# Query granules and gathered rows share a six-buffer ring: one ring of six becomes a pool of five and a pool of one, and row work begins within the second query granule

## Chip, cores and metric

The kernel runs on one core of a Trainium2 chip. The metric is the device time of one execution in microseconds (us). Before the change three runs took 1511.29 to 1512.45 us, median 1511.89 us.

## What is computed

Two transformer-like blocks on 256 tokens of width 1024, all in fp32. The first block has a mixer and a mixture of 32 experts. The second has two attentions and ends with a layer that picks, for each token, 128 of 16384 experts by product keys (16 for each of 8 heads) and applies them. Only that last layer is touched by what the change is about:

```python
q = (xt @ w_q).reshape(t, PEER_HEADS, 2, PEER_HALF)
sc = jnp.einsum("thpc,hpnc->thpn", q, sub_keys)
top_s, top_i = lax.top_k(sc, PEER_TOPK)
...
best_s, best_pos = lax.top_k(cand_s, PEER_TOPK)
idx = jnp.take_along_axis(cand_i, best_pos, axis=-1)
gate = jax.nn.softmax(best_s, axis=-1)
...
uc = u[ic]
act = jnp.einsum("cd,ced->ce", xc, uc)
hid = jax.nn.gelu(act) * gc
return jnp.einsum("ce,ced->cd", hid, v[ic])
```

## The kernel before, in words

**Weights.** All large weights are cut into granules of 128 x 4096 fp32 (2 MiB). `src` lists them in the order of use: 8 for the first mixer, 96 for the experts (two gates, two ups, two downs for each pair of experts), 17 for the second block, of which the last four are the query granules (`w_q`). A granule's load is issued by SyncE (SP) in `pump` (L298) as soon as its buffer is known to be free; `free` (L318) counts granules whose last piece has been split. Buffers come from a ring of six (`ring`), beside which a ring of three (`ring2`) serves during the first eight pairs of experts.

**Splitting.** Outside the experts each granule is used in pieces of 128 x 512. `chunk` (L197) splits a piece in two float32r parts: ScalarE (ACT) rounds the high part (L163), VectorE (DVE) or GpSimd (POOL) subtracts for the low part (L164), and TensorE (PE) multiplies both (L233). Pieces are split two ahead of their use. A query granule has eight pieces, so its last piece is split while its sixth is multiplied, and the next granule's first piece one step later.

**The last layer.** Four query granules are worked off one after the other (loop at the end of `_body`, `projT`, L225; here called the first to fourth granule, i = 0 to 3 in the code). After each, `scores` (L1326, L1328) multiplies with the keys, and `best` and `choose` (DVE, in small pieces) find the rows to gather: 32 per granule for the first 128 tokens, then 128 for the other tokens. `step` (L1238) emits one such piece of work and calls `fetch`.

**Rows.** For each of the 256 choices a *row tile half* is gathered: for each of 128 tokens one row of `uv`, 8 KiB, in all 1 MiB. Two gathers fill one 2 MiB buffer of the ring. `fetch` (L1228) issues them from POOL. In the code before, row buffers follow the granules in the same ring of six, in ring order: the first row pair takes the place of the sixth last granule, and so on, so the number of row pairs in flight is three during the second granule, four in the third, five in the fourth, six after it.

**Places.** `places` handles one pair of gathers at a time, here called a place: `first` twice (DVE, L1266, 128 x 1024 product with a sum), then `second` for both: Gelu (ACT, L1271), gate (L1273) and a diagonal matrix (L1275) for each, and matmuls that add the weighted rows to the result in PSUM (PE, L1278). When the matmuls of a place are done, its buffer is free and POOL issues the next pair of gathers. There are 128 places. Before the change, the first place comes with the first step of the third granule: `alongside` puts one place behind each of the nine steps of the third and of the fourth granule, and all others follow the fourth.

```python
def drive(main, fill, per):
    acc = 0.0
    for _ in main:
        acc += per
        while acc >= 1:
            acc -= 1
            next(fill, None)
```

The order of the instructions on each engine is the order in which this program emits them; an engine waits at its first instruction whose operands are not ready.

Of the kernel before, what the change touches and what calls it, by code (L numbers as in the profile page):

```python
# [1 line left out]

# [1 line left out]

# [4 lines left out]
F32 = mybir.dt.float32  # L9
# [22 lines left out]
NRING = 6  # L32
NRING2 = 3
# [20 lines left out]
RQ = 1.6  # L54
# [9 lines left out]
def _body(tc, A, out, dbg):  # L64
# [3 lines left out]
    def pool(name, bufs, **kw):  # L68
        return tc.tile_pool(name=name, bufs=bufs, reuse_waits="tile", **kw)
# [6 lines left out]
    with ExitStack() as ctx:  # L76
# [201 lines left out]
# [8 lines that stand above are left out]
# [3 lines left out]
        n_pre = len(src)  # L289
# [3 lines left out]
        src += [A["w_in2"][0], A["w_kv"]] + [A["w_in2"][i] for i in range(1, 8)] + [A["w_pa"], A["w_pb"]]  # L293
        src += [A["w_out2"][i] for i in range(2)] + [A["w_q"][i] for i in range(4)]
        st = {"emitted": 0, "freed": 0, "got": 0, "tiles": {}, "cap": 2, "next2": 0}
        R2_END = n_pre + 5 * (NRING + NRING2)

        def pump():  # L298
            while st["emitted"] < len(src) and st["emitted"] < st["freed"] + (NRING + NRING2 if rg[1] is not None and n_pre + NRING <= st["emitted"] < R2_END + NRING else st["cap"]):
                i = st["emitted"]  # L300
                if rg[1] is None and n_pre + NRING <= i < n_pre + NRING + NRING2:
                    break
                p = rg[1] if rg[1] is not None and n_pre <= i < R2_END and (i - n_pre) % (NRING + NRING2) >= NRING else rg[0]
                w = p.tile([128, 4096], F32, tag="w", name="w")
                n = src[i].shape[1]
                for o in range(0, n, 1024 if i == 0 else n):
                    v = slice(o, o + (1024 if i == 0 else n))
                    nc.sync.dma_start(w[:, v], src[i][:, v])
                st["tiles"][i] = w
                st["emitted"] += 1  # L310
# [10 lines left out]
                st["freed"] += 1  # L321
            pump()

        rg = [None, None]
        ringctx = ExitStack()
        rg[0] = ringctx.enter_context(pool("ring", NRING, side="right"))
        psctx = ExitStack()
        psx[0] = psctx.enter_context(pool("ps", 8, space=PSUM))
        pump()
# [24 lines left out]
        with pool("p1", 1) as p1:  # L354
# [3 lines left out]
            nc.sync.dma_start(kc2, A["kconst2"])  # L358
            nc.sync.dma_start(rr, row(A["grows"], R_END))
            nc.sync.dma_start(ws, A["w_s"])  # L360
            st["cap"] = NRING
            pump()
            nT = pp.tile([128, 2, 8, T], F32R, tag="xh", name="nT")
            warm(WARM[0])
# [277 lines left out]


        r2x = ExitStack()
        rg[1] = r2x.enter_context(pool("ring2", NRING2, side="right"))
        pump()
        xh = pp.tile([128, 2, 2, D], F32R, tag="xh", name="xh")
        if True:
# [70 lines left out]
            with pool("p2b", 2) as q, pool("p2c", 1) as q1:  # L719
# [76 lines left out]
                for p in range(16):  # L796
                    if p == 8:
                        r2x.close()
                        overflow(tc, nc, A, Pp, Wt, most, xh, res, gc, ident, bank, evac)
                        py = pyx.enter_context(pool("py", 1, side="right"))  # L800
                        fg = py.tile([128, D], F32, name="fg")
                        nc.gpsimd.dma_start(fg, row(A["final_gain"], D))
                        yy = py.tile([128, 2, D], F32, name="yy")
                        ss2 = py.tile([128, 2, 2], F32, name="ss2")
# [8 lines left out]
                    for dst in (pg, pu):  # L813
                        w = [get(), get()]
# [407 lines left out]
        todo = []  # L1222
        chosen = [0]
        got = {}
        row_st = {"next": 0, "done": 0}

        def fetch():

            while row_st["next"] < min(256, chosen[0]) and len(src) + row_st["next"] // 2 < st["freed"] + row_st["done"] // 2 + NRING:
                k = row_st["next"]  # L1230
                w = rg[0].tile([128, 4096], F32, tag="w", name="w")
                for j in range(2):
                    tt, s = divmod(k + j, 128)
                    got[k + j] = rw = w[:, j * 2 * D:(j + 1) * 2 * D]
                    nc.gpsimd.indirect_dma_start(rw, None, A["uv"], bass.IndirectOffsetOnAxis(ap=ei[tt][:, s:s + 1], axis=0))  # L1235
                row_st["next"] += 2
# [93 lines left out]
        def keep(qT, h0):  # L1330
            def f(hh, b):
                evac(flat(qT[:, h0 + 2 * hh:h0 + 2 * hh + 2, :]), b, eng="a")
            return f

        for i in range(4):
            qT = pq2.tile([128, 4, T], F32, name="qT")
            if i == 0:
                run(projT(8, n4, keep(qT, 0), 2))
                scores(0, qT, (0, 1))
                todo.append(seq(best(0, 0, (0, 1)), choose(0, 0, 1)))  # L1340
                lo_eng[0] = [nc.gpsimd]
                drive(projT(8, n4, keep(qT, 2), 2), fill, RQ)
                scores(0, qT, (2, 3))
                todo.append(seq(best(0, 0, (2, 3)), choose(0, 1, 1)))

                for tt in range(2):
                    for hf in range(2):
                        nc.tensor.matmul(acc[tt][hf], ident, res[:, tt, hf * 512:(hf + 1) * 512], start=True, stop=False, skip_group_check=True)
                continue
            drive(projT(8, n4, keep(qT, 0)), al if i > 1 else fill, 1 if i > 1 else RQ)  # L1350
            lo_eng[0] = [nc.vector]
            scores(i, qT, range(4))
            todo.append(seq(best(0, i), choose(0, 2 * i, 2)))
# [166 lines left out]
```

## Time and profile before

| | us |
|---|---|
| median of three runs | 1511.89 |
| the profiled execution | 1514.62 |
| its span in the trace | 1512.6 |
| PE busy | 1287.3 (85%) |
| DVE busy | 791.4 (52%) |
| ACT busy | 502.4 (33%) |
| POOL busy | 473.0 (31%) |
| DMA, mean rate over the span | 351 GB/s |

Busy time is that of instructions of an engine; waiting is not in it. The span runs from the first to the last instruction of the profiled execution, and the trace counts time from its start. The trace's mean shares hide that the program has stages with different limits: the experts run from about 150 to 610 us, the second block's attentions to about 795 us, the query granules from about 796 to 960 us, and the remaining rows to the end.

### The profile page before, as it was taken

The numbers are of one execution on the slowest core, as the hardware profiler recorded it, in microseconds if no ns is written. First come the engines' busy times: TensorE is split into PE (matmuls) and PEld (weight loads), VectorE is DVE, ScalarE is ACT, GpSimd is POOL, SyncE is SP. The second block draws the span as 40 slices with busy tenths as digits, with TensorE's granted clock in tenths as the row PEclk, the third lists the DMA queues.
The fourth block names the chain that finished last, engine by engine and source line by source line (L and its number), as shares of the span: only waits on it lengthen the run. The fifth ranks groups of instructions, "written<-read, shape, count | busy, mean of one in ns | idle before, by whom it ended". The sixth has DMA issues, their size and how long they took to land.

```text
span 1512.6 us, 16176 instructions
## 1 busy us (share of the span) xinstructions
PE 1287.3 (85%) x5523; PEld 703.8 (47%) x5523; DVE 791.4 (52%) x1797; ACT 502.4 (33%) x1211; POOL 473.0 (31%) x379
## 2 busy tenths in 40 slices
PE   9899999999899998999997878887777597777776
PEld 7676344334344453888886544433222232222222
DVE  4766222222222222677578667799874454544444
ACT  6635111011010012546654433444433232323332
POOL 1211000000000001243116343455566556665661
PEclk9999999999999999999998999999999999999999
DMA  9526799999999999644334698899999999999995
GB/s 390 225 112 278 312 426 428 426 428 426 428 428 427 429 427 427 265 177 147 115 123 162 241 399 303 358 422 422 421 421 421 421 422 421 422 422 421 421 422 237
DMA packets 57747, 530.21 MB, mean 351 GB/s; under 512 B 6592, under 2 KB 6848, under 8 KB 9408
## 3 DMA queue, kind: packets, MB, share of 16 engines
q0 software_dynamic: 37936, 272.65, 44.0%
q1 hardware_dynamic: 19440, 256.35, 40.7%
q8 instruction: 45, 0.74, 0.2%
q14 instruction: 38, 0.31, 0.1%
q10 hardware_dynamic: 288, 0.16, 0.0%
HBM read 528.08 MB, written 1.05 MB: 350 GB/s over the span
## 4 chain that ended last, share of the span: by engine, by line
DMA 27%; PE 12%; DVE 10%; issue 5%; ACT 3%; POOL 2%; POOLq 0%; DVEq 0%; ACTq 0%
DMA w<-in_uv_dram,ei 27%; PE b L233 6%; DVE jk L1266 5%; PE acc L1278 2%; PE b L262 1%; PE b L246 1%; POOL w L1235 1%; DVE sl L164 1%; ACT sh L163 1%; PE b L1030 1%; ACT dg L1275 1%; DVE oh L1186 1%; PE b L1016 0%; DVE en L1192 0%; PE b L976 0%
## 5 line engine op out<-in xcount | busy, mean ns | idle before, releaser
L1278 PE MATMUL acc<-w,dg 128*128 128x512 f32 x1024 | 479.5, 614 | 158.5 <-ACT dg L1275 158.2
L1235 POOL DMA_INDIRECT w<-in_uv_dram,ei x256 | 355.7, 1389 | 294.6 <-DMA w<-in_uv_dram,ei 131.7
L1266 DVE SCALAR_TENSOR_TENSOR jk<-w,xr 128x1024 f32<-128x1024 f32 x256 | 313.0, 1223 | 191.6 <-DMA w<-in_uv_dram,ei 189.8
L1278 PEld LDWEIGHTS acc<-w,dg 128*128 128x128 f32 x1024 | 188.8, 193 | 438.4 <-ACT dg L1275 244.0
L817 PE MATMUL b<-w,xg 128*64 128x512 f32 x1024 | 238.0, 601 | 11.9 <-DMA w<-in_w_gate_dram 9.6
L164 DVE TENSOR_TENSOR sl<-w,sh 128x512 fp32r<-128x512 f32 (+1 forms) x185 | 128.7, 702 | 105.6 <-ACT sh L163 105.1
L1271 ACT ACTIVATE act<-act,rr_n 128x2 f32<-128x2 f32 x129 | 38.1, 295 | 398.7 <-DVE jk L1266 398.5
L163 ACT ACTIVATE sh<-w 128x512 fp32r<-128x512 f32 (+1 forms) x208 | 122.3, 603 | 110.5 <-PE b L233 70.9
L817 PEld LDWEIGHTS b<-w,xg 128*64 128x64 f32 x1024 | 86.0, 138 | 151.9 <-issue 126.7
L811 POOL TENSOR_TENSOR Dw<-Dw,Wt 128x256 f32<-128x256 f32 x16 | 9.9, 617 | 391.1 <-DVE Dw L810 391.1
L855 PE MATMUL b<-w,hT 128*64 128x512 f32 x512 | 115.8, 595 | 6.3 <-ACT hT L124 5.5
L233 PE MATMUL b<-nT,sh 128*128 128x256 f32 x576 | 107.1, 286 | 3.2 <-ACT sh L163 1.7
L1275 ACT ACTIVATE dg<-kc,act 128x128 f32<-128x128 f32 x256 | 102.8, 401 | 8.3
L233 PEld LDWEIGHTS b<-nT,sh 128*128 128x128 f32 x576 | 88.9, 189 | 9.4 <-issue 4.7
L780 DVE TENSOR_TENSOR res<-res,b 128x512 f32<-128x512 f32 x64 | 39.9, 681 | 100.9 <-PE b L778 100.9
L233 PE MATMUL b<-nT,sl 128*128 128x256 f32 x288 | 81.9, 284 | 3.1 <-DVE sl L164 2.9
L860 DVE SCALAR_TENSOR_TENSOR eo<-b,gs,eo 128x512 fp32r<-128x512 f32 x32 | 24.0, 750 | 114.0 <-ACT eo L859 111.3
L1273 ACT ACTIVATE act<-act,gt 128x1 f32<-128x1 f32 x256 | 73.4, 287 | 4.2
L855 PEld LDWEIGHTS b<-w,hT 128*64 128x64 f32 x512 | 41.4, 137 | 68.1 <-issue 56.2
L824 DVE TENSOR_TENSOR hs<-hs,b 128x512 f32<-128x512 f32 x16 | 11.0, 688 | 106.4 <-PE b L817 106.4
L859 ACT ACTIVATE eo<-b,gs 128x512 fp32r<-128x512 f32 x32 | 22.0, 687 | 114.2 <-PE b L855 87.6
L246 PE MATMUL b<-sh,nT 128*128 128x512 f32 (+1 forms) x192 | 58.3, 380 | 0.5 <-ACT sh L163 0.5
(373 smaller groups left out, 1411.0 us busy)
## 6 DMA issues: line engine op xcount, KB each, us to landing
w<-in_w_gate_dram SPq DMA_DIRECT2D x32, 2048.0 KB, 19.1
w<-in_w_up_dram SPq DMA_DIRECT2D x32, 2048.0 KB, 21.3
w<-in_w_down_dram SPq DMA_DIRECT2D x32, 2048.0 KB, 19.1
w<-in_w_in_dram SPq DMA_DIRECT2D x13, 2048.0 KB, 16.7
w<-in_w_out_dram SPq DMA_DIRECT2D x4, 2048.0 KB, 13.2
w<-in_w_q_dram SPq DMA_DIRECT2D x4, 2048.0 KB, 7.9
w<-in_uv_dram,ei POOLq DMA_INDIRECT x256, 19.1
w<-in_w_in_dram SPq DMA_DIRECT2D x4, 512.0 KB, 7.1
```

Source lines behind the costliest of these rows:

```text
L163: nc.scalar.activation(hi, src, AF.Copy)
L164: (eng or nc.vector).tensor_tensor(lo, src, hi.bitcast(F32), op=ALU.subtract)
L233: nc.tensor.matmul(dst, l[:, c * 128:(c + 1) * 128], x[:, r, k, :], start=(k == 0 and c % 2 == 0 and i == 0), stop=(k == nk - 1 and i == 2 ...
L246: nc.tensor.matmul(bs[tt][:, :n], x[:, l, k, tt * 128:(tt + 1) * 128], r[:, :n], start=(k == 0 and i == 0), stop=(k == 7 and i == 2))
L780: nc.vector.tensor_tensor(rs, rs, b, op=ALU.add)
L817: nc.tensor.matmul(dst[64 * j:64 * j + 64, :], xg[:, k, 2 * pr + j, :], w[j][:, k * 512:(k + 1) * 512], start=(k == 0), stop=(k == 7))
L855: nc.tensor.matmul(bh[half][64 * j:64 * j + 64, :], hT[:, f, 64 * j:64 * j + 64], w[j][:, f * 1024 + half * 512:f * 1024 + half * 512 + 51 ...
L1235: nc.gpsimd.indirect_dma_start(rw, None, A["uv"], bass.IndirectOffsetOnAxis(ap=ei[tt][:, s:s + 1], axis=0))
L1266: nc.vector.scalar_tensor_tensor(junk, got[k][:, 0:D], 1.0, xr[:, tt], op0=ALU.mult, op1=ALU.mult, accum_out=act[tt][:, s:s + 1])
L1273: nc.scalar.activation(v[:, j:j + 1], v[:, j:j + 1], AF.Copy, scale=gf[tt][:, s + j:s + j + 1])
L1275: nc.scalar.activation(dg, ident, AF.Copy, scale=v[:, j:j + 1])
L1278: nc.tensor.matmul(acc[tt][hf], dg, rw[:, D + hf * 512:D + (hf + 1) * 512], start=False, stop=(s + j == 127), skip_group_check=True)
```

## The change

The ring of six becomes a pool of five (`ring`) and a pool of one (`ring1`); the three of `ring2` stay. `pool_of` says which granule lives where: during the first 45 expert granules the pattern of nine is five, one, three; elsewhere every sixth granule lives in the one. Of the last six granules, four live in the five, and the last two (the third and fourth query granules) both live in the one, so the fourth can only be loaded when the third has been split. Row pairs live in the five; once all granules are freed, every sixth pair lives in the one. `space` decides from counts of freed granules and finished rows whether a buffer may be taken. And in the second granule the steps are driven otherwise: four steps with two pieces of choosing each, then the other four steps and the end with 0.7 places each, which makes three places.

```diff
+        N_THREE = 45
+
+        def pool_of(i):
+
+            j = i - n_pre
+            if 0 <= j < N_THREE:
+                return 2 if j % 9 > 5 else 1 if j % 9 == 5 else 0
+            if i >= len(src) - 6:
+                return 1 if i >= len(src) - 2 else 0
+            return 1 if (i if j < 0 else j - N_THREE) % 6 == 5 else 0
+
+        held = [[], [], []]
+        size = (NRING - 1, 1, NRING2)
+        row_st = {"next": 0, "done": 0}
+
+        def space(p):
+            if rg[p] is None:
+                return False
+            if len(held[p]) < size[p]:
+                return True
+            x = held[p][-size[p]]
+            return x < st["freed"] if x >= 0 else 2 * (-1 - x) + 2 <= row_st["done"]
 
         def pump():
-            while st["emitted"] < len(src) and st["emitted"] < st["freed"] + (NRING + NRING2 if ... else st["cap"]):
+            while st["emitted"] < len(src) and st["emitted"] < st["freed"] + st["cap"]:
                 i = st["emitted"]
-                if rg[1] is None and n_pre + NRING <= i < n_pre + NRING + NRING2:
+                p = pool_of(i)
+                if not space(p):
                     break
...
-        rg[0] = ringctx.enter_context(pool("ring", NRING, side="right"))
+        rg[0] = ringctx.enter_context(pool("ring", NRING - 1, side="right"))
+        rg[1] = ringctx.enter_context(pool("ring1", 1, side="right"))
...
-            st["cap"] = NRING
+            st["cap"] = NRING + NRING2
...
         def fetch():
 
-            while row_st["next"] < min(256, chosen[0]) and len(src) + row_st["next"] // 2 < st["freed"] + row_st["done"] // 2 + NRING:
+            while row_st["next"] < min(256, chosen[0]):
                 k = row_st["next"]
-                w = rg[0].tile([128, 4096], F32, tag="w", name="w")
+
+                p = 1 if st["freed"] == len(src) and k % 12 == 10 else 0
+                if not space(p):
+                    break
+                held[p].append(-1 - k // 2)
+                w = rg[p].tile([128, 4096], F32, tag="w", name="w")
...
-            drive(projT(8, n4, keep(qT, 0)), al if i > 1 else fill, 1 if i > 1 else RQ)
+            if i == 1:
+                main = projT(8, n4, keep(qT, 0))
+                drive(itertools.islice(main, 4), fill, 2)
+                drive(main, al, 0.7)
+            else:
+                drive(projT(8, n4, keep(qT, 0)), al, 1)
```

What moves in the order of the instructions, at three places. First SP, the loads of the query granules (before, then after; in brackets what a load waits for; `w_5603` and `w_6653` are the buffers of the fourth granule):

```order
L308 DMA w_4813<-in_w_out2_dram 128x4096 [waits DMAHW4_49,DVE_49]
L308 DMA w_5062<-in_w_q_dram 128x4096 [waits DMAHW5_49,DVE_49]
L308 DMA w_5296<-in_w_q_dram 128x4096 [waits DMAHW6_49,DVE_49]
L308 DMA w_5463<-in_w_q_dram 128x4096 [waits DMAHW7_49,DVE_49]
L308 DMA w_5603<-in_w_q_dram 128x4096 [waits DMAHW0_49,DVE_49]
```

```order
L331 DMA w_4816<-in_w_out2_dram 128x4096 [waits DMAHW4_49,DVE_49]
L331 DMA w_5065<-in_w_q_dram 128x4096 [waits DMAHW5_49,DVE_49]
L331 DMA w_5464<-in_w_q_dram 128x4096 [waits DMAHW7_49,DVE_49]
L331 DMA w_5466<-in_w_q_dram 128x4096 [waits DMAHW6_49]
L331 DMA w_6653<-in_w_q_dram 128x4096 [waits DMAHW5_49,DVE_49,Pool_49]
```

The order of the loads stays, but the fourth granule's now waits for the DVE split of the last piece of the third granule (`w_5466`).

Second POOL, from the first gathers to the end of the second granule (`sl` is the low part of a piece; before, then after):

```order
L1235 DMA w_6155<-in_uv_dram,ei0_5863 128x2048 x2
L164 TENSOR_TENSOR sl_6175<-w_5296,sh_6174 128x512
L164 TENSOR_TENSOR sl_6195<-w_5296,sh_6194 128x512
L164 TENSOR_TENSOR sl_6217<-w_5296,sh_6216 128x512
L164 TENSOR_TENSOR sl_6240<-w_5296,sh_6239 128x512
L164 TENSOR_TENSOR sl_6265<-w_5296,sh_6264 128x512
L164 TENSOR_TENSOR sl_6290<-w_5296,sh_6289 128x512
L1235 DMA w_6307<-in_uv_dram,ei0_5863 128x2048 x2
L164 TENSOR_TENSOR sl_6311<-w_5463,sh_6310 128x512
L164 TENSOR_TENSOR sl_6331<-w_5463,sh_6330 128x512
L1235 DMA w_6398<-in_uv_dram,ei0_5863 128x2048 x2
```

```order
L1263 DMA w_6159<-in_uv_dram,ei0_5864 128x2048 x2
L165 TENSOR_TENSOR sl_6179<-w_5464,sh_6178 128x512
...
L165 TENSOR_TENSOR sl_6278<-w_5464,sh_6277 128x512
L165 TENSOR_TENSOR sl_6294<-w_5464,sh_6293 128x512
L1263 DMA w_6324<-in_uv_dram,ei0_5864 128x2048 x2
L1263 DMA w_6327<-in_uv_dram,ei0_5864 128x2048 x2
L165 TENSOR_TENSOR sl_6333<-w_5466,sh_6332 128x512
L1263 DMA w_6364<-in_uv_dram,ei0_5864 128x2048 x2
L165 TENSOR_TENSOR sl_6371<-w_5466,sh_6370 128x512
L1263 DMA w_6407<-in_uv_dram,ei0_5864 128x2048 x2
```

Ahead of the second granule's splits there are now four pairs of gathers and not three, and four further pairs are issued before the third granule begins, where there was one.

Third ACT, the end of the second granule (`sh` is the high part of a piece, `qT` the granule's result, `sc` the scores, `act0` and `dg` belong to a place; before, then after):

```order
L163 ACTIVATE sh_6289<-w_5296 128x512
L163 ACTIVATE sh_6310<-w_5463 128x512
L163 ACTIVATE sh_6330<-w_5463 128x512
L124 ACTIVATE qT_6171<-b_6172 128x512
L124 ACTIVATE qT_6171<-b_6173 128x512
L1328 ACTIVATE sc_5887<-b_6352,rr_n4_5916 128x512
L1328 ACTIVATE sc_5887<-b_6358,rr_n4_5916 128x512
L163 ACTIVATE sh_6367<-w_5463 128x512
L1271 ACT_TABLE_LOAD
L1271 ACTIVATE act0_5867<-act0_5867,rr_n4_5916 128x2
```

```order
L164 ACTIVATE sh_6293<-w_5464 128x512
L1299 ACT_TABLE_LOAD
L1299 ACTIVATE act0_5868<-act0_5868,rr_n4_5917 128x2
...
L164 ACTIVATE sh_6332<-w_5466 128x512
L1299 ACTIVATE act0_5868<-act0_5868,rr_n4_5917 128x2
...
L164 ACTIVATE sh_6370<-w_5466 128x512
L125 ACTIVATE qT_6175<-b_6176 128x512
L125 ACTIVATE qT_6175<-b_6177 128x512
L1299 ACTIVATE act0_5868<-act0_5868,rr_n4_5917 128x2
...
L1356 ACTIVATE sc_5888<-b_6410,rr_n4_5917 128x512
L1356 ACTIVATE sc_5888<-b_6416,rr_n4_5917 128x512
L164 ACTIVATE sh_6425<-w_5466 128x512
```

Three places now stand before the scores of the second granule, the third of them between the copy of its result and the scores.

## Rows read from the trace of the kernel before

**Rows 1.** Page, the span in 40 slices: rate of the DMA.
```profile
GB/s 390 225 112 278 312 426 428 426 428 426 428 428 427 429 427 427 265 177 147 115 123 162 241 399 303 358 422 422 421 421 421 421 422 421 422 422 421 421 422 237
```
**Rows 2.** Busy time by stage: stretch, length, engines, PE clock, DMA share, GB/s.
```profile
818.00:841.00 23.00, 19.48 (x118) 17.23 (x117) 13.07 (x46) 6.90 (x13) 17.94 (x17) 0.85 0.80 308
841.00:901.00 60.00, 49.35 (x199) 29.41 (x198) 41.06 (x115) 25.89 (x64) 24.22 (x21) 0.97 0.81 315
901.00:960.00 59.00, 47.19 (x176) 26.96 (x174) 40.59 (x117) 22.31 (x58) 21.06 (x20) 0.94 0.88 347
975.00:1480.00 505.00, 379.66 (x822) 149.23 (x821) 313.79 (x712) 176.13 (x529) 299.02 (x206) 0.99 1.01 420
```
**Rows 3.** Timeline of POOL late in the rows: start, length, operation.
```profile
1138.15 1.87 POOL L1235 DMA_INDIRECT w<-in_uv_dram,ei  x1 [0.62 <-DMA w<-in_uv_dram,ei]
...
1143.12 1.87 POOL L1235 DMA_INDIRECT w<-in_uv_dram,ei  x1 [0.61 <-DMA w<-in_uv_dram,ei]
```
**Rows 4.** Timeline of ACT, second to fourth granule; in brackets the idle time before.
```profile
834.77 0.63 ACT L163 ACTIVATE sh<-w 128x512 fp32r<-128x512 f32 x1 [1.35 <-PE b L233]
...
838.43 1.31 ACT L124 ACTIVATE qT<-b 128x512 f32<-128x512 f32 x2
...
842.66 1.28 ACT L1271 ACT_TABLE_LOAD   x1
845.81 0.30 ACT L1271 ACTIVATE act<-act,rr_n 128x2 f32<-128x2 f32 x1 [1.87 <-DVE jk L1266]
...
846.46 0.40 ACT L1275 ACTIVATE dg<-kc,act 128x128 f32<-128x128 f32 x1
...
873.10 0.61 ACT L163 ACTIVATE sh<-w 128x512 fp32r<-128x512 f32 x1
...
879.36 0.61 ACT L163 ACTIVATE sh<-w 128x512 fp32r<-128x512 f32 x1
...
906.19 0.29 ACT L1271 ACTIVATE act<-act,rr_n 128x2 f32<-128x2 f32 x1 [4.98 <-DVE jk L1266]
```
**Rows 5.** Timeline of DVE, first step of the third granule.
```profile
842.67 0.69 DVE L164 TENSOR_TENSOR sl<-w,sh 128x512 fp32r<-128x512 f32 x1 [7.96 <-ACT sh L163]
843.28 1.22 DVE L1266 SCALAR_TENSOR_TENSOR jk<-w,xr 128x1024 f32<-128x1024 f32 x1
```
**Rows 6.** Timeline of POOL: first gather, sixth gather, splits of the second granule.
```profile
818.43 1.05 POOL L1235 DMA_INDIRECT w<-in_uv_dram,ei  x1 [0.16 <-DVE gt L1198]
...
825.46 0.94 POOL L1235 DMA_INDIRECT w<-in_uv_dram,ei  x1 [0.30 <-issue]
826.42 3.74 POOL L164 TENSOR_TENSOR sl<-w,sh 128x512 fp32r<-128x512 f32 x3
```
**Rows 7.** Timeline of PE: the second granule's last matmul.
```profile
838.83 0.28 PE L233 MATMUL b<-n,sl 128*128 128x256 f32 x1
```
**Rows 8.** Chain that ended last, in order of time: start, length, what.
```profile
690.06 3.06 PE b L233 x24
...
872.63 3.70 PE acc L1278 x8
891.05 7.13 PE acc L1278 x16
```
**Rows 9.** DMA issues: KB each, median us to landing; page, then 877.5 to 880 us.
```profile
w<-in_w_q_dram SPq DMA_DIRECT2D x4, 2048.0 KB, 7.9
w<-in_uv_dram,ei POOLq DMA_INDIRECT x2, 11.0
```
**Rows 10.** Timeline of SP and busy time by stage, before the experts.
```profile
121.08 7.75 SPq L308 DMA_DIRECT2D w<-in_w_down_dram  x2
150.00:155.00 5.00, 5.00 (x32) 3.73 (x33) 2.08 (x5) 1.23 (x4) 0.44 (x1) 0.87 0.02 7
```
**Rows 11.** Timeline of DVE: two casts of row numbers, 128 x 16.
```profile
816.96 0.17 DVE L1193 CAST ei<-en 128x16 int32<-128x16 f32 x1
...
826.43 3.77 DVE L1193 CAST ei<-en 128x16 int32<-128x16 f32 x1
```

More of the change, by code (lines that the diff above doesn't have):

```diff
@@ L1 @@
 from contextlib import ExitStack
+import itertools
 import numpy as np
@@ L295, in _body @@
         st = {"emitted": 0, "freed": 0, "got": 0, "tiles": {}, "cap": 2, "next2": 0}
-        R2_END = n_pre + 5 * (NRING + NRING2)
+        N_THREE = 45
[16 more added lines that the diff above has]
+            return x < st["freed"] if x >= 0 else 2 * (-1 - x) + 2 <= row_st["done"]
         def pump():
-            while st["emitted"] < len(src) and st["emitted"] < st["freed"] + (NRING + NRING2 if rg[1] is not None and n_pre + NRING <= st["emitted"] < R2_END + NRING else st["cap"]):
+            while st["emitted"] < len(src) and st["emitted"] < st["freed"] + st["cap"]:
                 i = st["emitted"]
-                if rg[1] is None and n_pre + NRING <= i < n_pre + NRING + NRING2:
+                p = pool_of(i)
+                if not space(p):
                     break
-                p = rg[1] if rg[1] is not None and n_pre <= i < R2_END and (i - n_pre) % (NRING + NRING2) >= NRING else rg[0]
-                w = p.tile([128, 4096], F32, tag="w", name="w")
+                held[p].append(i)
+                w = rg[p].tile([128, 4096], F32, tag="w", name="w")
                 n = src[i].shape[1]
@@ L322, in free @@
             pump()
-        rg = [None, None]
+        rg = [None, None, None]
         ringctx = ExitStack()
-        rg[0] = ringctx.enter_context(pool("ring", NRING, side="right"))
+        rg[0] = ringctx.enter_context(pool("ring", NRING - 1, side="right"))
+        rg[1] = ringctx.enter_context(pool("ring1", 1, side="right"))
         psctx = ExitStack()
@@ L644, in _body @@
         r2x = ExitStack()
-        rg[1] = r2x.enter_context(pool("ring2", NRING2, side="right"))
+        rg[2] = r2x.enter_context(pool("ring2", NRING2, side="right"))
         pump()
@@ L798, in _body @@
                         r2x.close()
+                        rg[2] = None
                         overflow(tc, nc, A, Pp, Wt, most, xh, res, gc, ident, bank, evac)
@@ L1224, in _body @@
         got = {}
-        row_st = {"next": 0, "done": 0}
         def fetch():
-            while row_st["next"] < min(256, chosen[0]) and len(src) + row_st["next"] // 2 < st["freed"] + row_st["done"] // 2 + NRING:
+            while row_st["next"] < min(256, chosen[0]):
                 k = row_st["next"]
-                w = rg[0].tile([128, 4096], F32, tag="w", name="w")
+                p = 1 if st["freed"] == len(src) and k % 12 == 10 else 0
+                if not space(p):
+                    break
+                held[p].append(-1 - k // 2)
+                w = rg[p].tile([128, 4096], F32, tag="w", name="w")
                 for j in range(2):
```

## Prediction

> **What bounds the kernel now.** The page's 40 slices come first: the DMA runs near 425 GB/s through the experts, falls to 115 to 240 in the attentions, and from slice 27 on is level at 421 to 422 until the last [rows 1]. So the end is set by gathers, and the question is when they become an unbroken stream. The busy times by stage answer it: in the second granule (818 to 841 us) the DMA is busy 0.80 of the time, in the third 0.81, in the fourth 0.88, and from 975 us on 1.01 [rows 2]. Late in the rows POOL issues one pair of gathers per 1143.12 - 1138.15 = 4.97 us, and each issue was released by an earlier gather's landing [rows 3]. A pair that is ahead when the stream becomes unbroken is therefore worth 4.97 us, and a microsecond by which this moment comes later costs a microsecond.
>
> What sets the pace until then is no engine's busy time: PE is busy 49.35 of 60 us, DVE 41.06, ACT 25.89 [rows 2]. The timelines show a ring of waits. DVE does `first` twice (1.22 us each) [rows 5], ACT then Gelu, gates and diagonals of the place and only behind them the high part of the next piece, DVE the low part (0.69) behind that [rows 5], and the next `first` stands behind the low part. High parts come 879.36 - 873.10 = 6.26 us apart [rows 4]. A place within a granule so costs some 6.3 us against the 4.97 that its gathers need: that is where the DMA's idle time in the third and fourth granule comes from.
>
> The trace is of an execution of 1514.62 us (span 1512.6), 2.7 above the median 1511.89. I work out a difference on the trace and add it to the median. A measurement can tell about 0.2% (3 us) from no change.
>
> **What the change gains.** Places are counted from 0. Before, 18 stand in the third and fourth granule, and the gather that opens the unbroken stream waits for the first place behind them (18). With six pairs in flight 24 pairs have been issued by then. Now 3 + 9 + 9 = 21 places stand in the granules; the fourth granule still reaches six in flight (five, and the one when the last granule is split), so 27 pairs have been issued. Gain: 3 x 4.97 = **14.9 us**, if place 21 came when place 18 came.
>
> **What it costs: three places in the second granule.**
> - POOL issues eight gathers and not six before that granule's splits. The six took from 818.43 to 826.40, 1.33 each [rows 6]; two more are 2.7 us, and PE waits for the split behind them. PE's sixth step, two steps (3.06 us [rows 8]) before the end at 839.1 [rows 7], moves from 836.0 to 838.7.
> - ACT's last high part of the granule moves from 834.77 to 837.5 and ends at 838.1; a table load of 1.28 follows, then Gelu, gate and diagonal, 1.05 us from the first to the second's start plus its length [rows 4]: PE starts place 0 at about 840.4. A place is 3.70 us on PE [rows 8], a step 1.53. Place 0, step 7, place 1, step 8: 840.4 + 3.70 + 1.53 + 3.70 + 1.53 = 850.9.
> - Place 2 stands behind the copy of the result (1.31) [rows 4] and its own 1.05, then 3.70: 857.0.
> - From the last matmul of a granule's last place to the next granule's first Gelu the trace has 891.05 + 7.13 = 898.2 to 906.19 [rows 4, 8], 8.0 us: scores, their copies, a split, the first search, `first` twice. So the third granule's first Gelu comes at 865.0. Before it comes at 845.81 [rows 4].
>
> The third granule begins **19.2 us** late. From there on the instructions are the same, nine places per granule. As lower end I take PE's time of the three places alone, 11.1 us, all else hidden; as upper end 19.2 plus six `first` of 1.22 that hide nowhere, 26.5. I take 19.2, since it is the sum of rows in the order in which the engines must run them.
>
> **The last granule's load.** It was issued in the attentions, long before use; now it waits for the low part of the third granule's last piece. That piece's high part stands behind the third granule's fifth place, ACT's next high part, 6.26 us later, is already the new granule's first. High 0.61 and low 0.69 leave 6.26 - 1.30 = 5.0 us for a load. A 2 MiB load of this line lands after 7.9 us with little beside it; gathers issued in the same stretch as this load land after up to 11.0 [rows 9]. That bounds the wait at 2.9 and 6.0 us; with a whole pair of gathers before it (4.97 more) at 11.0. I take 9.5 to land, midway between the two rows: a wait of **4.5 us**. Behind it on ACT stands the next place's Gelu, on DVE the low part and all later `first`, so nothing of the ring of waits goes on. PE has two steps and the last place left, and gathers already issued go on landing: this costs no bandwidth, only time to the stream.
>
> The Trainium skill, *DMA: Bandwidth & Descriptors*, Anatomy of one DMA, gives 2.0 us plus bytes over 436 GB/s, an estimate of 6.8 us for this load; its section Queues, rings and completion order says that the DMA engines take turns between SP's and POOL's queues packet by packet, so a load would share and not queue. By the fit alone the wait would be 1.8 us and the sum 2.7 lower; the 7.9 us row is what I hold to as the lower end.
>
> **What costs nothing.** The pool split also delays two early loads. The fourth expert granule takes its buffer from the sixth weight before the experts and now from the seventh: it goes out at 121.08 [rows 10], when the fifth went out before. From there the loads behind it follow within 8 us, and the DMA's idle stretch after them (0.02 busy in 150 to 155 us [rows 10]) takes up the one load more, 4.97 us at most. Later the patterns of nine and of six give each granule the buffer of the same predecessor as before. The second and third query granules are loaded a little later or together, in the attentions, where the DMA is at 115 to 240 GB/s [rows 1]. Of these I book 0, at most 5 if the idle stretch were gone.
>
> **Sum.** 19.2 + 4.5 - 14.9 = +8.8 us. On the median: 1511.9 + 8.8 = **1520.7 us**, slower.
>
> **Rivals.**
> - *Faster: the three places hide in waits.* From 834.7 to 842.67 DVE waits 7.96 us for ACT [rows 5], and the DMA idles a fifth of the second and third granule [rows 2]. If the places used only such waits, the lag would be PE's 11.1 us less some 4.5 in which PE stands still at the turn to the third granule (an estimate from its 49.35 of 60 us [rows 2], of which I give this turn under half), 6.6; with the low wait of 2.9: 6.6 + 2.9 - 14.9 = -5.4, 1506.5 us. It decides at the third granule's first Gelu: before 845.8 + 14.9 - 4.5 = 856.2 us the change gains. Against it: PE runs its instructions in order, and the eight steps, three places and the scores stand on it one behind the other.
> - *No change: the lag is some 15 us and the load lands early.* 15.0 + 2.9 - 14.9 = +3.0 at most, about 1513.
> - *Slower still: DVE and POOL in each other's way.* A cast that takes 0.17 us took 3.77 while POOL split three pieces, 826.42 to 830.16 [rows 6, 11]: DVE ended when POOL did. Now six `first` and the second choice stand on DVE while POOL splits the rest of the second granule and two pieces of the third. If each `first` cost its 1.22 us on the path once, 7.3 more: 1528.0. The Trainium skill, *SBUF — State Buffer*, Who interferes with whom, says that a DVE instruction with two inputs in SBUF contends with a GpSimd instruction that reads SBUF, the later one being blocked for the whole of the other; by that rule `first` is such an instruction and this rival holds, and the sum would be 16.1 rather than 8.8. Against it: POOL's splits are spread over the granule and PE, not DVE, is the longer line in it.
> - *Slower still: the load queues behind gathers.* Wait 11.0 instead of 4.5: 1527.2. For it: five pairs may be outstanding. Against it: in these granules the DMA is idle a fifth of the time [rows 2], so the queue is short.
>
> **How the numbers follow.** Forecast (1515 to 1526) 0.60; no change 0.14; faster 0.11; contention 0.10; queued load 0.05. Slower in all: 0.60 + 0.10 + 0.05 = 0.75. The range leaves out most of the faster case and the far ends of the two slower ones: 1510 to 1528 us. Its ends lie inside the extremes 11.1 + 2.9 - 14.9 = -0.9 and 26.5 + 11.0 - 14.9 = +22.6, which would need all unknowns on one side; the lower is stretched by a microsecond towards the faster rival.
>
> **What would show it.** In the new trace the three places' matmuls should lie between about 840 and 857 us and the third granule's first Gelu at 865; the DMA should be busy over 0.9 from 820 to 857 (0.80 before). On ACT a wait of 3 to 6 us for the fourth granule's load should stand behind the third granule's sixth place, near 898 us. The unbroken stream should begin near 998 us, 24 later than before, with 54 gathers behind it and not 48. The forecast is wrong if the first Gelu comes before 856 or no wait for the load is seen on ACT; it is wrong in its logic if the stream's start is as late as I say and the end is not.

## The result, and the profile after

After the change four runs took 1524.70 to 1525.13 us, median 1524.82; the kernel before, beside them, had a median of 1512.17. The ratio is 1.0082, with a 95% interval of 1.0064 to 1.0099: 12.65 us slower. The profiled execution took 1524.70 us (span 1522.9), 10.1 more than the profiled one of before, which lay 2.5 above its median. The forecast was 1520.7 us, slower, in 1510 to 1528.

In the profile after, everything up to the first gather of the rows is 1.8 us earlier than in the one of before (816.62 against 818.43 [rows 6]). Differences "from the first gather" below leave this offset out.

Rate by slices (page), and busy time by stage with the columns of [rows 2]:

```profile
GB/s 390 221 56 320 348 428 428 426 427 426 428 427 427 428 428 427 247 179 151 77 66 220 292 344 270 357 416 422 420 421 422 421 421 421 421 422 421 422 421 216
```

```profile
818.00:841.00 23.00, 15.63 (x85) 12.39 (x84) 18.89 (x47) 8.11 (x18) 20.58 (x15) 0.85 0.94 370
841.00:860.00 19.00, 13.32 (x69) 9.08 (x67) 4.17 (x16) 5.19 (x11) 8.50 (x9) 0.98 0.98 407
860.00:900.00 40.00, 32.66 (x120) 18.79 (x120) 25.91 (x81) 14.97 (x38) 12.80 (x12) 0.92 0.78 296
900.00:922.00 22.00, 14.19 (x35) 6.99 (x36) 10.96 (x19) 6.96 (x19) 4.27 (x5) 0.77 0.68 273
980.00:998.00 18.00, 12.49 (x38) 6.18 (x37) 13.59 (x61) 5.17 (x15) 5.81 (x6) 0.91 1.02 421
998.00:1490.00 492.00, 370.93 (x802) 145.40 (x800) 309.58 (x711) 172.38 (x518) 287.69 (x202) 0.99 1.01 421
```

The DMA is busy 0.94 to 0.98 up to 860 us, where it was 0.80 [rows 2]; it falls to 0.78 and 0.68 in the third granule and is unbroken (1.02) only from about 980 us on. The timeline of ACT shows why; it answers to [rows 4]: the three new places' Gelus, the third granule's first and sixth, the first split of the fourth granule, the seventh Gelu, the fourth granule's first:

```profile
836.30 0.29 ACT L1299 ACTIVATE act<-act,rr_n 128x2 f32<-128x2 f32 x1
...
838.40 0.28 ACT L1299 ACTIVATE act<-act,rr_n 128x2 f32<-128x2 f32 x1
...
847.94 0.29 ACT L1299 ACTIVATE act<-act,rr_n 128x2 f32<-128x2 f32 x1
...
860.75 0.30 ACT L1299 ACTIVATE act<-act,rr_n 128x2 f32<-128x2 f32 x1 [4.98 <-DVE jk L1294]
...
893.26 0.30 ACT L1299 ACTIVATE act<-act,rr_n 128x2 f32<-128x2 f32 x1 [4.07 <-DVE jk L1294]
...
900.96 0.63 ACT L164 ACTIVATE sh<-w 128x512 fp32r<-128x512 f32 x1 [6.03 <-DMA w<-in_w_q_dram]
...
906.70 0.29 ACT L1299 ACTIVATE act<-act,rr_n 128x2 f32<-128x2 f32 x1 [5.11 <-DVE jk L1294]
...
930.89 0.29 ACT L1299 ACTIVATE act<-act,rr_n 128x2 f32<-128x2 f32 x1 [4.99 <-DVE jk L1294]
```

Two late points stand in it. The third granule's first Gelu comes 44.13 us after the first gather (860.75 - 816.62) and not 27.38 [rows 4, 6]: a lag of **16.8 us**. And the third granule is 70.14 us long (to 930.89), not 60.38 [rows 4]: **9.8 us** more, most of it at 900.96, where ACT waits 6.03 us for the fourth granule's load. PE's clock goes down behind the wait: 0.77 in 900 to 922 us. On SP the load goes out at 889.97 us, and right behind it the load of the last norm's gain, which before had been issued at 769 us:

```profile
889.97 0.33 SPq L331 DMA_DIRECT2D w<-in_w_q_dram  x1
890.49 0.33 SPq L1389 DMA_DIRECT2D fg<-in_norm_f_dram  x1
```

Last, the issues of gathers. In the kernel before, the pair that opens the unbroken stream (24, counted from 0) and the last gather:

```profile
971.50 1.53 POOL L1235 DMA_INDIRECT w<-in_uv_dram,ei  x1 [11.49 <-PE acc L1278]
...
1480.21 1.88 POOL L1235 DMA_INDIRECT w<-in_uv_dram,ei  x1 [0.61 <-DMA w<-in_uv_dram,ei]
```

After the change (pair 27, and the last):

```profile
995.06 1.74 POOL L1263 DMA_INDIRECT w<-in_uv_dram,ei  x1 [10.02 <-DVE cand L1183]
...
1488.82 1.88 POOL L1263 DMA_INDIRECT w<-in_uv_dram,ei  x1 [0.61 <-DMA w<-in_uv_dram,ei]
```

The stream opens 23.56 us later with three pairs more issued. 23.56 - 3 x 4.97 = 8.65, and the last gather is 8.61 us later: the lateness of the stream's start less the pairs that are ahead is the whole difference up to there. Only the span behind the last gather is not in this account: 34.1 us here, 32.4 before. The 1.7 us lie in the last 16 matmuls, which take 8.83 us here and 7.13 before; the granted clock is 0.69 in 1506 to 1511 us, where it was 1.00 in that place before (1498 to 1506 us). In the four kernels of the next part that hold parts of the change the span behind the last gather is 32.4 to 32.5 us, but in the changed kernel with another order of splitting it is 34.2, with the same 8.83. Whether these 1.7 us belong to the change or to single executions is open.

### The profile page after: what moved, and what is told of

It is laid out like the page before. It is cut to its first block, busy times and chain, and to the rows that moved or that the text cites. A ratio compares the mean times of both kernels' runs of the same rounds, so it can differ in the third digit from the quotient of the medians.

```text
span 1522.9 us, 16160 instructions
## 1 busy us (share of the span) xinstructions
PE 1291.2 (85%) x5523; PEld 700.9 (46%) x5523; DVE 791.1 (52%) x1797; ACT 502.3 (33%) x1211; POOL 468.0 (31%) x379
## 4 chain that ended last, share of the span: by engine, by line
DMA 28%; PE 13%; DVE 9%; issue 5%; ACT 3%; POOL 2%; POOLq 0%; DVEq 0%; ACTq 0%; SPq 0%
DMA w<-in_uv_dram,ei 28%; PE b L234 6%; DVE jk L1294 4%; PE acc L1306 3%; PE b L263 1%; PE b L247 1%; POOL w L1263 1%; DVE sl L165 1%; DMA w<-in_w_q_dram 1%; ACT sh L164 1%; DVE en L1217 1%; PE b L1055 1%; DVE oh L1211 1%; ACT dg L1303 0%; PE b L1041 0%
## 5 line engine op out<-in xcount | busy, mean ns | idle before, releaser
L1306 PE MATMUL acc<-w,dg 128*128 128x512 f32 x1024 | 485.1, 620 | 164.4 <-ACT dg L1303 164.0
L1263 POOL DMA_INDIRECT w<-in_uv_dram,ei x256 | 346.6, 1354 | 313.2 <-DMA w<-in_uv_dram,ei 123.8
L842 PEld LDWEIGHTS b<-w,xg 128*64 128x64 f32 x1024 | 82.7, 139 | 155.1 <-issue 132.7
```

The costliest lines, as they stand in the source:

```text
L842: nc.tensor.matmul(dst[64 * j:64 * j + 64, :], xg[:, k, 2 * pr + j, :], w[j][:, k * 512:(k + 1) * 512], start=(k == 0), stop=(k == 7))
L1306: nc.tensor.matmul(acc[tt][hf], dg, rw[:, D + hf * 512:D + (hf + 1) * 512], start=False, stop=(s + j == 127), skip_group_check=True)
```

## The experiments

The theory when they began: the three early places cost about what they win; the loss comes from the fourth granule's late load. The rivals: the places themselves, or DVE and POOL in each other's way. All medians stand beside runs of the kernel before on the same chip; the experiments ran in three groups, in which it took 1512.75, 1511.98 and 1513.25 us.

### The pools alone

```diff
-            if i == 1:
-                main = projT(8, n4, keep(qT, 0))
-                drive(itertools.islice(main, 4), fill, 2)
-                drive(main, al, 0.7)
-            else:
-                drive(projT(8, n4, keep(qT, 0)), al, 1)
+            drive(projT(8, n4, keep(qT, 0)), al if i > 1 else fill, 1 if i > 1 else RQ)
```

> The pools of five and one as changed, but no places in the second granule: it is driven as before (1.6 pieces of choosing per step), the first place comes with the third granule. Theory (the loss is the last granule's late load; three early places cost about what they gain): the wait for that load stays, 6 us on ACT behind the third granule's sixth place, with some 2.6 us of slower TensorE after it, and no pair is gained: 24 pairs at the start of the unbroken stream. The third granule's first Gelu is 0 to 3 us later than before (two more gathers on POOL ahead of the splits). About 1512.2 + 9.8 = 1522 us, 1519 to 1525. Rival (the loss is the lag that the early places make): without them about the time before, 1511 to 1515 us, the wait for the load being taken back by the gathers that go on landing meanwhile.

Measured: 1523.52 us, ratio 1.0081 (1.0062 to 1.0100). ACT's timeline (the third granule's first Gelu, the fourth's first split):

```profile
846.50 0.29 ACT L1299 ACTIVATE act<-act,rr_n 128x2 f32<-128x2 f32 x1 [1.87 <-DVE jk L1294]
...
887.66 0.63 ACT L164 ACTIVATE sh<-w 128x512 fp32r<-128x512 f32 x1 [7.53 <-DMA w<-in_w_q_dram]
```

The third granule begins on time (26.5 us from the first gather, 820.04, against 27.4) and is 69.45 us long. Without a single early place all of the loss is there: the pools alone cost what the whole change costs.

### The places alone

The kernel before, its ring of six kept:

```diff
-            drive(projT(8, n4, keep(qT, 0)), al if i > 1 else fill, 1 if i > 1 else RQ)
+            if i == 1:
+                main = projT(8, n4, keep(qT, 0))
+                drive(itertools.islice(main, 4), fill, 2)
+                drive(main, al, 0.7)
+            else:
+                drive(projT(8, n4, keep(qT, 0)), al, 1)
```

> The ring of six of the kernel before, with the new driving of the second granule: three places in it, the fourth granule's load issued long before use. Theory: no wait for a load; the third granule's first Gelu comes some 17 us later against its first gather, 27 pairs stand at the start of the stream: 16.8 - 14.9 = +1.9 us against before, 1514 us, 1512 to 1517 (the upper end if the longer tail, 1.7 us, belongs to the places). Rival (the places themselves lose, by contention of DVE and POOL or by an order that hides nothing): 1520 to 1525 us. Second rival (with three pairs in flight instead of four in the second granule the third place has its gathers late): the first Gelu of the third granule over 20 us later than before.

Measured: 1516.07 us, ratio 1.0016 (1.0006 to 1.0027), +2.4 us by the ratio. ACT's timeline, the third granule's first, sixth and seventh Gelu:

```profile
860.57 0.30 ACT L1273 ACTIVATE act<-act,rr_n 128x2 f32<-128x2 f32 x1 [4.99 <-DVE jk L1268]
...
893.63 0.29 ACT L1273 ACTIVATE act<-act,rr_n 128x2 f32<-128x2 f32 x1 [4.08 <-DVE jk L1268]
...
900.93 0.30 ACT L1273 ACTIVATE act<-act,rr_n 128x2 f32<-128x2 f32 x1 [5.11 <-DVE jk L1268]
```

From the first gather (818.36) the first Gelu comes after 42.21 us, a lag of 14.8, against a gain of 14.9: the three places cost what they gain. Most of the +2.4 lies inside the third granule, which is 61.99 us long, 1.6 more than before. The sixth and the seventh Gelu are 7.30 us apart here and 13.44 after the change: the difference, 6.14, is ACT's wait for the load (6.03). The lag is 2 us shorter than after the change; six gathers and not eight stand ahead of the splits on POOL here.

### The last granule in the five, and the gain's load first

The first of these two keeps the third granule in the one and puts the fourth into the five, so that it loads early; a pool's held buffers are counted, so that rows may pass the granules:

```diff
-                return 1 if i >= len(src) - 2 else 0
+                return 1 if i == len(src) - 2 else 0
...
-            if len(held[p]) < size[p]:
-                return True
-            x = held[p][-size[p]]
-            return x < st["freed"] if x >= 0 else 2 * (-1 - x) + 2 <= row_st["done"]
+            return sum(x >= st["freed"] if x >= 0 else 2 * (-1 - x) + 2 > row_st["done"] for x in held[p]) < size[p]
```

> As changed, but only the third granule lives in the one; the fourth is loaded into the five, early. A pool's buffers are counted as free when fewer than its number are held, whatever their order. One pair fewer is in flight in the second, third and fourth granule (three, four, four instead of four, five, five). Theory: no wait for the fourth granule's load, the third granule is 60 and not 70 us long: 1524.8 - 9.8 = 1515 us, 1513 to 1518. Rival (four pairs in flight are too few for a place per 6.3 us, so what the load gives back the gathers take): the first places of the fourth granule wait for gathers and the time stays above 1520 us.

Measured: 1515.31 us, ratio 1.0020 (1.0012 to 1.0029). Taking the late load away gives back 9.4 us of the 12.65 (1.0082 - 1.0020 of 1512), although one pair fewer is in flight, and the lag is 14.0 (first Gelu at 860.77, first gather at 819.43). Its profiled execution (1520.15 us) lies 4.8 above its own median, with a place of 6.72 us on PE in the third granule; I read no lengths of that granule from it.

The second moves the load of the last norm's gain (`fg`, two lines) ahead of the loop over the granules:

> As changed, but the load of the last norm's gain (512 KB), which stands on SP directly behind the fourth granule's late load, is issued ahead of that load, before the query granules are worked off. Theory: the two loads shared the DMA; alone the granule lands up to 0.5 MB / 421 GB/s = 1.2 us earlier: the wait on ACT is 4.8 to 5.6 us and not 6.0, the time 1523.5 to 1524.5 us. Rival (the load is slow by the gathers beside it and its own length alone): wait and time as they are, within 0.3 us.

Measured: 1524.33 us, ratio 1.0082 (1.0069 to 1.0096). SP's and ACT's timelines:

```profile
806.25 0.33 SPq L1364 DMA_DIRECT2D fg<-in_norm_f_dram  x1
...
888.98 0.33 SPq L331 DMA_DIRECT2D w<-in_w_q_dram  x1
```

```profile
899.29 0.63 ACT L164 ACTIVATE sh<-w 128x512 fp32r<-128x512 f32 x1 [5.35 <-DMA w<-in_w_q_dram]
```

The wait is 5.35 and not 6.03 us: 0.7 shorter, within the theory's 4.8 to 5.6. The medians, 0.5 us apart, are too near to tell.

### What sets the pace in the granules

The prediction had said that a ring of waits does: DVE's `first`, ACT's Gelu and behind it the next high part, DVE's low part, the next `first`. Five kernels try it. Three have the next piece split between the two `first` and the Gelu (the body of `chunk`'s loop becomes `split_next`):

```diff
+        def split_ahead():
+            if cs["i"] < len(cs["q"]) and len(cs["ready"]) <= cs["look"]:
+                cs["ready"].append(split_next())
...
                         first(k + i)
+                    split_ahead()
                     second(k + j, n)
```

On the kernel before:

> The kernel before, with one change of order: within a place, the next piece of the query granule is split (high part on ACT, low part on DVE) between the two first and the Gelu, not behind the Gelu, gates and diagonals. Theory (a place within a granule costs 6.3 us because ACT's high part stands behind the Gelu, which waits for both first, and DVE's low part waits for that high part; PE needs only 3.70 + 1.53 = 5.23): DVE no longer waits for ACT, a place costs 5.2 to 5.5 us, the 18 places of the third and fourth granule take some 18 x 0.9 = 16 us less, the unbroken stream begins that much earlier: 1512.2 - 16 = 1496 us, 1493 to 1504. Rival (PE or the landing of the gathers sets the pace of the places): 1509 to 1514 us. Second rival (the high part, now ahead of the Gelu, delays the place's matmuls by its 0.6 us and takes back what it gives): 1510 to 1516 us.

With the ring of six and the three early places:

> The ring of six of the kernel before, the new driving with three places in the second granule, and the split between the two first and the Gelu. Theory: the gain of that order as in the kernel before with it, and three places at about their price: within 3 us of the run of the kernel before with that order, 1494 to 1505 us. Rival (three early places pay once the granules are faster, since PE is then the bound and a place costs 5.2 us against the 4.97 us of its gathers): no, they would then lose up to a microsecond less; below that run by more than 3 us would show that the lag in the second granule came from the same order of ACT and DVE.

On the kernel as changed:

> The kernel as changed, with the split between the two first and the Gelu. Theory: the fourth granule's load is still issued only when the third granule's last piece is split and still needs some 10 us to land; the place that hides part of it is shorter, so the wait is 6 to 8 us; the places gain as in the other kernels with that order: 8 to 12 us above the run with the ring of six, the new driving and that order. Rival (the wait for the load came of the order of ACT and DVE): within 4 us of that run.

Measured: 1521.17 (ratio 1.0057, 1.0043 to 1.0071), 1522.40 (1.0072) and 1534.09 us (1.0143). My expectation failed: the order made all three slower. Of the comparisons among the three, those that were expected hold: the places cost 1.2 us, the late load another 11.7. ACT's wait for that load is 9.37 us in the third of them, longer than the 6 to 8 expected. ACT's timeline of the first shows what happened:

```profile
859.13 0.28 ACT L1278 ACTIVATE act<-act,rr_n 128x2 f32<-128x2 f32 x1
...
865.28 0.63 ACT L163 ACTIVATE sh<-w 128x512 fp32r<-128x512 f32 x1 [4.48 <-PE b L240]
865.81 0.28 ACT L1278 ACTIVATE act<-act,rr_n 128x2 f32<-128x2 f32 x1
```

There are three buffers for high parts; with one more piece kept ready the new one takes the buffer of the step that PE has just been given, so ACT waits 4.48 us for that step, and the Gelu stands behind it: a place costs 6.68 us. The fourth kernel takes the low parts of the last two granules from DVE instead:

```diff
-            lo_eng[0] = [nc.vector]
             scores(i, qT, range(4))
```

> The kernel before, with the low parts of the third and fourth granule on POOL instead of DVE. Theory (the ring of waits of ACT and DVE sets the pace): DVE's first no longer wait for the low parts, PE sets the pace with 5.2 us per place, 1496 to 1506 us, if POOL's low parts (1.3 us each) leave DVE alone. Rival (DVE and POOL are in each other's way): a first beside a low part of POOL takes up to twice its 1.22 us and POOL's issues of gathers stand behind its low parts, 1512 to 1520 us.

Measured: **1493.95 us**, ratio 0.9877 (0.9860 to 0.9893). That leaves two readings (order, or less work on DVE), so the kernel before with `split_ahead` was tried again, with a piece less kept ready:

```diff
+            if i > 1:
+                cs["look"] = 1
             drive(projT(8, n4, keep(qT, 0)), al if i > 1 else fill, 1 if i > 1 else RQ)
```

> The kernel before with the next split between the two first and the Gelu, as in the earlier run with that order, but in the third and fourth granule one piece fewer is kept ready, so that the split finds one of the three buffers free and ACT's high part does not wait for the step just ahead of it on PE. Theory (the ring of waits from DVE's first over ACT's high part to DVE's low part sets the pace, and the earlier run lost only because the high part waited 4.48 us for PE's step, with the Gelu behind it): 4.9 to 5.3 us per place, as with the low parts on POOL, 1493 to 1500 us. Rival (taking the low parts from DVE was what helped, its busy time and not the order): 6 us per place and more, 1508 to 1516 us.

Measured: **1493.90 us**, ratio 0.9875 (0.9858 to 0.9892). The low parts are still on DVE, and the gain is the same: DVE's load need not fall for it, the new order is enough. What keeping one piece fewer ready does without the new order was not run. Timelines of PE, with the low parts on POOL, and of ACT and the stages, with the new order:

```profile
865.09 3.60 PE L1278 MATMUL acc<-w,dg 128*128 128x512 f32 x8
...
869.95 3.60 PE L1278 MATMUL acc<-w,dg 128*128 128x512 f32 x8
```

```profile
863.16 0.30 ACT L1278 ACTIVATE act<-act,rr_n 128x2 f32<-128x2 f32 x1 [2.00 <-DVE jk L1273]
...
868.11 0.29 ACT L1278 ACTIVATE act<-act,rr_n 128x2 f32<-128x2 f32 x1 [2.07 <-DVE jk L1273]
```

```profile
841.00:860.00 19.00, 18.64 (x76) 11.08 (x75) 18.69 (x67) 10.47 (x26) 8.78 (x7) 1.00 0.73 271
860.00:900.00 40.00, 36.10 (x144) 21.37 (x143) 32.41 (x98) 17.38 (x46) 17.71 (x17) 0.96 1.01 416
900.00:925.00 25.00, 25.00 (x108) 15.41 (x107) 23.05 (x44) 13.04 (x32) 13.68 (x13) 1.00 1.01 417
```

A place comes every 4.86 us with the low parts on POOL and every 4.95 with the new order (868.11 - 863.16), PE has no gap between places in the last stretch (25.00 of 25 us busy), and the DMA is full from 860 us on and not from 975. Both beat the kernel before by 18 to 19 us; the two changes weren't joined.

### The changed kernel and its places at this pace

Low parts on POOL (the same line left out), first with the ring of six and the early places, then in the kernel as changed:

> The ring of six, the new driving with three places in the second granule, and the low parts of the third and fourth granule on POOL. Theory: with a place per 4.9 us the gathers are the bound from the third granule on, so a place more in the second granule moves no gather but those ahead of the turn; the eighth pair is issued at 868.4 us with the ring of six and these places, at 864.1 us in the kernel before with low parts on POOL: 1494 + 4 = 1498 us, 1494 to 1502. Rival (27 pairs instead of 24 at the stream's start are worth their 14.9 us whatever the pace): 1483 to 1490 us.

> The kernel as changed, with the low parts of the third and fourth granule on POOL. Theory: the wait for the fourth granule's load is still there on ACT (5 to 8 us), but with a place per 4.9 us five pairs in flight are mostly not landed yet, some 20 us of gathers, so the DMA does not idle and the wait costs nothing at the end: 1493 to 1499 us, no later than the ring of six with the same places and low parts on POOL. Rival (the wait adds its length whatever the pace): 7 to 10 us above that run, 1503 to 1509 us.

Measured: 1496.06 us (ratio 0.9890, 0.9872 to 0.9909) and 1512.28 us (0.9997, 0.9988 to 1.0006). The first is as the theory had it, 2.1 above the kernel without early places. For the second the theory failed; the wait does add its length, as the rival had it, but it is 15.78 us long, and the late load costs 16.2. ACT's and POOL's timelines:

```profile
902.80 0.63 ACT L164 ACTIVATE sh<-w 128x512 fp32r<-128x512 f32 x1 [15.78 <-DMA w<-in_w_q_dram]
```

```profile
887.25 0.95 POOL L1263 DMA_INDIRECT w<-in_uv_dram,ei  x1 [0.83 <-PE acc L1306]
888.50 0.94 POOL L1263 DMA_INDIRECT w<-in_uv_dram,ei  x1 [0.30 <-issue]
889.46 1.27 POOL L165 TENSOR_TENSOR sl<-w,sh 128x512 fp32r<-128x512 f32 x1
```

The third granule's last low part now stands on POOL behind two gathers that waited for PE; the buffer is free at 890.7, 3.7 us after ACT had come to the next piece (887.0), and the load is in use from 902.8. Pair 14 is issued at 911.10, 19 us behind pair 13: five pairs in flight didn't cover the stop. In 900 to 925 us the DMA's share is 0.81, where it is 0.99 with the ring of six and the same places and low parts.

## Why the prediction was right, point by point

- **Gain, 14.9 us: right.** 27 pairs were issued when the stream opened, and 23.56 - 14.9 is the lateness of the last gather to 0.1 us. The gather of pair 27 at 995.06 us and 54 gathers before it are what the forecast named (near 998, with an offset of 1.8).
- **Lag, 19.2 us: right in kind, 2.4 too long.** Measured 16.8. The last step, 8.0 us from place 2's matmuls to the next Gelu, held: they end at 849.04 + 3.70 = 852.74, the Gelu comes at 860.75. The steps ahead of it were too long; PE's timeline of the three places:

```profile
837.41 3.70 PE L1306 MATMUL acc<-w,dg 128*128 128x512 f32 x8 [1.28 <-ACT dg L1303]
...
842.38 3.60 PE L1306 MATMUL acc<-w,dg 128*128 128x512 f32 x8
...
849.04 3.70 PE L1306 MATMUL acc<-w,dg 128*128 128x512 f32 x8 [1.63 <-ACT dg L1303]
```

  With the offset of 1.8 taken off, I had place 0 at 838.6 and place 2 at 851.5. Place 0 came 1.2 earlier. From place 0 to place 1 it is 4.97 us, not 3.70 + 1.53 = 5.23: the matmuls of place and step overlap, which a sum of durations doesn't show. The last stretch, from place 1 to place 2, was 1.0 shorter than my sum. The two kernels with early places and six gathers ahead of the splits have lags of 14.8 and 14.0, this one and the one with the gain first, with eight, 16.8 and 16.7: these 2 us are POOL's two gathers more (my term: 2.7). Its splits begin 10.20 us behind the first gather (826.82 - 816.62), where they began after 7.99 [rows 6].
- **The last granule's load, 4.5 us: right in its place, too small.** ACT's wait stands behind the sixth place, as named, and is 6.03 us. The 5.0 us that I had as free were there (issued at 889.97, wanted at 894.93); too short was the term for landing, 11.0 us until ACT could read and not 9.5. Of that, 0.7 is a step that I missed: the gain's load moved on SP to right behind the blocked one and shares the DMA with it. I also ended the price with the wait. Behind it PE's clock was lower (last section), and the last two Gelus of the granule are 4.46 us apart (912.07, 916.53) where they were 2.53: with the wait, the third granule is 8.15 us longer than in the run of the places alone. That run has 1.6 more than before for another reason, which I booked at nothing when I wrote that from there on the instructions are the same: the steps of choosing fall on other places. A high part now stands behind one of their table loads on ACT (fifth Gelu 7.80 us behind the fourth, 6.25 before), and a reduction of 1.81 us between a low part and the `first` (seventh behind the sixth 7.30, 6.27 before); other intervals are shorter.
- **"This costs no bandwidth, only time to the stream": right as an account.** The last gather is late by the stream's lateness less the three pairs; what landed during the wait gave nothing back. As a picture of the DMA it is too mild: five pairs did not outlast the wait, and in 910 to 914 us the DMA is busy 0.01. The kernel with the fourth granule in the five, without the wait, is 9.4 us faster.
- **Early loads, 0: right.** The idle stretch took them up: the DMA is busy 0.68 in 150 to 155 us, where it was 0.02 [rows 10], and the first gather is not later.
- **Sum.** From the first gather: 16.75 (lag) + 9.76 (third granule) + 0.33 (fourth) - 1.47 (the pair that opens the stream follows its Gelu after 6.47 us, not 7.94) - 14.91 = +10.46; the last gather is 10.42 later by that count. Forecast 8.8. With the tail (1.7) and without the offset (1.8) that is the 10.3 between the spans. The other 2.4 of the 12.65 is the height of the profiled execution of before over its median; where it lies within that execution is open. That the sum comes so near is luck in part: the lag was 2.4 too long, and the third granule, for which only the load's 4.5 stood in the sum, 5.3 too short.
- **Rivals.** The faster one needed the third granule's first Gelu before 856.2; it came at 860.75. DVE and POOL did get in each other's way (below), but in two of the six `first` only, and the lag came out shorter than forecast, not longer. The load queued behind gathers only in part: 11.0 us, between the 9.5 that I took and this rival's 16.
- **The ring of waits: right as a mechanism, and worth more than the change.** An order that breaks it, or low parts on POOL, gives 18 to 19 us.

## What to carry to other kernels

Before starting work earlier, look at what paces the stage it comes from: three places ahead were worth 14.9 us and cost as much, one instruction order on ACT and DVE was worth 18 to 19. A buffer that is given to other data turns a load with ample time into one with a deadline: count from the last reader of the old contents to the first of the new, with all that queues behind the blocked issue, and look at what stands ahead of the instruction that frees the buffer (the wait was 6 us here, and 16 where that instruction stood on POOL behind two gathers). An order that splits earlier needs a buffer free for it; count them first.

## What was not expected of the hardware

- **A 2 MiB load beside gathers.** From issue to its first reader it took 11.0 us after the change, 12.5 with the pools alone, 10.3 with the gain's load first, 11.6 with the earlier split and 12.0 with low parts on POOL, against a median of 7.9 [rows 9]. The Trainium skill, *DMA: Bandwidth & Descriptors*, Anatomy of one DMA, has its 2.0 us plus bytes over 436 GB/s, an estimate of 6.8 us for 2 MiB, for transfers that GpSimd issues. This load is issued by SP and runs beside gathers, so the page's figure was not made for it, in the prediction either, and the measurement decides.
- **DVE and POOL.** Timelines after the change, DVE and then POOL, while POOL split the second granule:

```profile
831.16 2.30 DVE L1294 SCALAR_TENSOR_TENSOR jk<-w,xr 128x1024 f32<-128x1024 f32 x1
...
833.51 2.19 DVE L1294 SCALAR_TENSOR_TENSOR jk<-w,xr 128x1024 f32<-128x1024 f32 x1
```

```profile
826.82 11.23 POOL L165 TENSOR_TENSOR sl<-w,sh 128x512 fp32r<-128x512 f32 x6
```

  Two of the six `first` take 2.30 and 2.19 us instead of 1.22 (the other four 1.21 to 1.23), and a split takes 11.23 / 6 = 1.87 instead of 1.28: both lose. The Trainium skill, *SBUF — State Buffer*, Who interferes with whom, says so of such a pair (the later waits for the other); the trace agrees, since 2.30 - 1.22 = 1.08 is less than one split. With low parts on POOL in the third and fourth granule, where one split falls to a place, the time nevertheless fell by 18 us.
- **The clock behind a wait.** PE stood still for 8.31 us ahead of the seventh place; its timeline and the busy time of the stretch (columns as in [rows 2]):

```profile
907.81 6.77 PE L1306 MATMUL acc<-w,dg 128*128 128x512 f32 x8 [8.31 <-ACT dg L1303]
```

```profile
901.00:916.00 15.00, 8.19 (x21) 4.34 (x22) 10.96 (x19) 4.86 (x13) 0.94 (x1) 0.66 0.56 236
```

  The granted clock is 0.66 of 2.4 GHz on average over this stretch; it falls while PE stands still (1.00 in 898 to 902 us, 0.72 in 902 to 906), is 0.50, which is 1.2 GHz, in 906 to 914 and 1.00 again in 914 to 918. The place takes 6.77 us instead of 3.70, a little under twice as long. So a wait of 6 us cost 8.
